# Block inverses of a gated delta rule: DMA re-layout replaced by VectorE's 32x32 transposes, and the order of queued matmuls written down

## The chip, the cores and the metric

One core of one Trainium2 chip runs the whole program in a single launch. The metric is the device time of one execution in microseconds. The kernel before took 2575.57 us (median of 3 runs, 2575.21 to 2578.09).

## The reference

Two layers over 512 latent tokens and 256 context tokens, model width 1024. Each layer: a modulated RMS norm, one input projection of 7696 columns, three mixers that run on its output (a gated convolution with 31 taps, neighbourhood attention, and a bidirectional gated delta rule, "GDN"), a gated merge with an output projection, then a second norm and a convolutional FFN of width 2816. What the change touches is the GDN's triangular solve:

```
lmat  = where(strict, (k*beta) @ k.T * decay, 0)        # decay = exp(g_i - g_j), lower triangle
sol   = triangular_solve(lmat, [v*beta, k*beta*exp(g)], lower=True, unit_diagonal=True)
a     = where(incl, q @ k.T * decay, 0)
# then a scan over chunks with the state s; both directions; 4 heads of 128
```

The kernel works with chunks of 128 tokens, so it has 6 chunks, 2 directions and 4 heads: 48 unit triangular matrices of 128x128 per layer. It inverts them explicitly.

## The kernel before

**Numbers.** Weights and activations of the large projections are split into a rounded high part and a low rest (fp32r, `whi`/`wlo` and `hl`/`ol`), and every product is three matmuls. A weight unit is fetched by SP (`raw`), rounded by ScalarE (`whi`, line 131) and subtracted by VectorE (`wlo`, line 132; the function `wunit`). Two raw and three high and low buffers rotate, so the rounding of a unit waits until TensorE has used the unit three before it.

**Order of a layer.** First the output gate and the decays' projection (`og_first` in layer 0, `og_proj` in layer 1), then `gates`, `gdn_proj` (q, k, v), then two calls of `gdn_core`, one for each pair of heads, then attention, merge, output projection and FFN.

**Queued work.** The projections of attention (`na_units`), of the convolution (`conv_a_proj`) and of the merge gate (`mg_units`) are generators in a queue. The code of the serial parts calls `fill(us)` between its steps, which issues queued matmuls of about that many nominal microseconds (columns x matmuls / 2400) from the queue; the constants stand in the table `FILL`, one row a layer. What is not used up there is issued later, in `finish`. The framework orders each engine's instructions at compile time; `tc.issue_after(ins)` makes the instructions of a block stand behind `ins` on the same engine, and without it a queued matmul may stand earlier or later than where it is written.

**GDN of one pair.** `gdn_core` loads rows of cumulated decays (`D`, lines 897 to 902), forms on VectorE the differences with the column and on ScalarE the exponential, multiplies the products `kk` with beta and decay into `E` (line 913; 24 matrices of 128x128: 12 a direction) and `qk` with decay into `Am`. `gdn_inverse` (line 1022) then inverts all 24. The four diagonal blocks of 32x32 of each are inverted by forward substitution with one matrix per partition: 4 x 12 = 48 matrices of the forward direction in partitions 0 to 47 and 48 of the backward direction, flipped, in 64 to 111. To bring a block of 32 partitions into one partition it goes through HBM: 4 DMAs write the blocks of `E` to `d_e` (line 1032), two read them back (1033, 1034), one loads identities (1036). 31 steps of two VectorE instructions follow (1042, 1044). Then two ScalarE copies with transposed reading (1047, 1048), a flip, four DMAs out (1051, 1052) and eight back (`Td`, line 1059, and the diagonal of `E`, line 1060). Matmuls then combine blocks of 32 to 64 (`iy`, `it`, `ir`, lines 1070 to 1083) and of 64 to 128 (1102, 1111), with evictions between and `fill` calls behind: `sub` behind the substitution, `y32`, `t32`, `y64`, `t64` behind the later steps.

**Taps.** The 31-tap convolution is 120 VectorE instructions `ca` (line 520) a layer, written in the attention's loop and tied behind marks: the first ones behind the end of a substitution, the rest behind the end of the second `gdn_core`.

**Norms.** `norm_mean` sums squares by matmuls of one column and takes a reciprocal square root in eleven small VectorE instructions; `norm_row` spreads it over partitions by matmuls; `norm_scale` and `norm_shift` apply it. Where a second stream's loop runs, `norm_apply` returns the steps as a list (`late`), and the loops take one a step.

## Time and profile before

| | |
|---|---|
| median of 3 runs | 2575.57 us (2575.21 to 2578.09) |
| the profiled execution | 2584.95 us, span 2583.2 us |
| mean granted TensorE clock | 0.982 |
| TensorE / VectorE / ScalarE busy | 96% / 72% / 42% |
| DMA | 356.74 MB, 138 GB/s on average |

The profile is of one execution. Busy is the share of the span in which an engine had an instruction; TensorE's clock is granted at full speed (2.4 GHz) or half of it, and a stretch's value is the mean of the two. A wait is put down to what ended last before the instruction could start.

### The profile page before, as it was taken

The page shows a single profiled execution, that of the slowest core. Times are in us where ns is not written, and L with a number is a line of the kernel's source. Part 1 is how long each engine was busy: PE and PEld are TensorE (multiplying, and loading weights), DVE is VectorE, ACT ScalarE, POOL GpSimd, SP SyncE. Part 2 cuts the span into 40 slices and gives each one's busy share as a digit, 9 for nine tenths or more (in the row PEclk, how much of TensorE's full clock was granted, in tenths as well). Part 3 has the DMA queues.
Part 4 walks back from the last instruction along what each step waited for, and adds up shares of the span by engine and source line. Part 5 has one row for each costly group of instructions (what it writes and reads, how often), then busy time and mean ns, then how long its engine had stood idle before and what let it go on. Part 6 is the DMA issues. An engine that isn't in the chain of part 4 may idle for free. (4 is left out here: it accounts for less than half of the span.)

```text
span 2583.2 us, 42109 instructions
## 1 busy us (share of the span) xinstructions
PE 2484.5 (96%) x16079; PEld 2160.4 (84%) x16079; DVE 1865.7 (72%) x4138; ACT 1072.2 (42%) x2159; POOL 8.5 (0%) x32
## 2 busy tenths in 40 slices
PE   6999999999999999999999999998988999999999
PEld 4988898977778888888888898888877778888887
DVE  5686478799679989877666578876767968755463
ACT  4574343455332344223233346634344544533242
POOL 0000000000000000000000000000000000000000
PEclk9999999999999999999999989998999999999999
DMA  7224434263458554444432342343446276323322
GB/s 254 93 82 127 133 101 139 95 210 103 147 189 265 186 160 134 132 143 129 153 120 89 119 147 83 133 131 109 145 124 216 90 238 203 126 90 99 97 98 90
DMA packets 206762, 356.74 MB, mean 138 GB/s; under 512 B 54320, under 2 KB 102688, under 8 KB 206432
## 3 DMA queue, kind: packets, MB, share of 16 engines
q1 hardware_dynamic: 181664, 320.97, 39.1%
q10 hardware_dynamic: 24896, 33.09, 3.6%
q8 instruction: 126, 2.06, 0.3%
q14 instruction: 76, 0.62, 0.1%
HBM read 297.31 MB, written 56.68 MB: 137 GB/s over the span
## 5 line engine op out<-in xcount | busy, mean ns | idle before, releaser
L131 ACT CAST whi<-raw 128x1024 fp32r<-128x1024 f32 (+2 forms) x319 | 331.6, 1040 | 564.0 <-PE dn L151 202.1
L132 DVE TENSOR_TENSOR wlo<-raw,whi 128x1024 fp32r<-128x1024 f32 (+2 forms) x319 | 385.4, 1208 | 188.1 <-ACT whi L131 185.3
L151 PE MATMUL upl<-hl,whi 128*128 128x512 f32 (+1 forms) x728 | 279.0, 384 | 2.9 <-ACT whi L131 2.0
L151 PE MATMUL upl<-ol,whi 128*128 128x512 f32 (+1 forms) x728 | 279.2, 384 | 0.0
L151 PE MATMUL upl<-hl,wlo 128*128 128x512 f32 (+1 forms) x728 | 278.4, 383 | 0.3 <-DVE wlo L132 0.3
L520 DVE SCALAR_TENSOR_TENSOR ca<-yp,caw,ca 128x783 f32<-128x783 f32 (+1 forms) x240 | 213.0, 887 | 8.1 <-ACT ca L513 6.0
L449 PE MATMUL pjl<-hl,whi 128*128 128x512 f32 x512 | 210.2, 411 | 4.1 <-ACT whi L131 4.1
L449 PE MATMUL pjl<-ol,whi 128*128 128x512 f32 x512 | 206.4, 403 | 0.0
L449 PE MATMUL pjl<-hl,wlo 128*128 128x512 f32 x512 | 204.7, 400 | 0.5 <-DVE wlo L132 0.5
L151 PEld LDWEIGHTS upl<-hl,whi 128*128 128x128 f32 x728 | 137.3, 189 | 28.7 <-ACT whi L131 2.2
L151 PEld LDWEIGHTS upl<-hl,wlo 128*128 128x128 f32 x728 | 137.2, 189 | 27.3 <-DVE wlo L132 0.5
L151 PEld LDWEIGHTS upl<-ol,whi 128*128 128x128 f32 x728 | 137.4, 189 | 25.1 <-DVE ol L324 0.2
L151 PE MATMUL dn<-fhl,wlo 128*128 128x512 f32 x352 | 139.5, 396 | 0.0
L151 PE MATMUL dn<-fll,whi 128*128 128x512 f32 x352 | 139.5, 396 | 0.0
L151 PE MATMUL dn<-fhl,whi 128*128 128x512 f32 x352 | 139.2, 396 | 0.0
L449 PEld LDWEIGHTS pjl<-hl,whi 128*128 128x128 f32 x512 | 97.5, 190 | 25.3 <-ACT whi L131 6.1
L246 DVE CUSTOM_DVE_ANT_1 aj<-at,crows,par 128x512 f32<-128x512 f32 x128 | 93.5, 748 | 33.4 <-DMA at<-ada_t 22.3
L449 PEld LDWEIGHTS pjl<-hl,wlo 128*128 128x128 f32 x512 | 97.4, 190 | 21.2 <-DVE wlo L132 0.9
L585 PE MATMUL na<-wlo,hl 128*128 128x256 f32 x384 | 110.0, 287 | 4.8 <-DVE wlo L132 2.6
L449 PEld LDWEIGHTS pjl<-ol,whi 128*128 128x128 f32 x512 | 97.8, 191 | 19.2 <-issue 0.8
L585 PE MATMUL na<-whi,ol 128*128 128x256 f32 x384 | 110.1, 287 | 0.0
L585 PE MATMUL na<-whi,hl 128*128 128x256 f32 x384 | 109.8, 286 | 0.0
(405 smaller groups left out, 6454.3 us busy)
## 6 DMA issues: line engine op xcount, KB each, us to landing
raw<-w_b SPq DMA_DIRECT2D x88, 512.0 KB
raw<-f_up SPq DMA_DIRECT2D x88, 512.0 KB
at<-ada_t SPq DMA_DIRECT2D x160, 256.0 KB
raw<-w_o SPq DMA_DIRECT2D x32, 512.0 KB
raw<-f_dn SPq DMA_DIRECT2D x32, 448.0 KB
raw<-w_a SPq DMA_DIRECT2D x24, 512.0 KB
mg<-mge ACTq DMA_DIRECT2D x48, 256.0 KB
raw<-w_br SPq DMA_DIRECT2D x24, 512.0 KB
```

What stands on the lines that cost most here:

```text
L131: self.nc.scalar.copy(hi[:, :n], r[:, :n])
L132: self.split = self.nc.vector.tensor_sub(lo[:, :n], r[:, :n], hi[:, :n]).ins
L151: self.nc.tensor.matmul(o, wk[a], x[k][b], start=(k == 0 and i == 0), stop=(k == n - 1 and i == 2))
L246: V.tensor_tensor_reduce(p, w, self.crows[:, r, 4 * h:4 * h + 4], 1.0, m if h else self.p(l, "adab")[:, t:t + 1], ALU.mult, ALU.add, accum ...
L449: self.nc.tensor.matmul(o, wk[a], x[k][b], start=(k == 0 and i == 0), stop=(k == n - 1 and i == 2))
L520: nc.vector.scalar_tensor_tensor(a, y[:, k:k + n], w[:, 31 * c + k:31 * c + k + 1], a, ALU.mult, ALU.add)
L585: self.nc.tensor.matmul(ps[:, :256], x[k][a], wk[b], start=(k == 0 and j == 0), stop=(k == 7 and j == 2))
```

## The change

In the inverse, no DMA is left. `V.transpose` transposes blocks of 32x32 between partitions and elements, so a block of `E` is brought into "one matrix per partition" by one block transpose of each group of 32 partitions (the backward direction; the forward direction by a ScalarE copy, so that both become lower triangular) and one transpose of the whole tile. The identities come from two memsets. After the substitution two transposes give both layouts of the inverse, `X` and `Yt`, which the matmuls of the 32-to-64 step read directly, with a step of 32 elements; the diagonal of `E` is filled by eight VectorE copies. `norm_row` is put behind the last matmul like `norm_mean`. The 31 steps are as before, on 128 partitions. The steps of 32 and of 64 run in two halves of six chunks each, each followed by a fill `inv`. All these matmuls, the fills `inv` and the norms' matmuls are issued in written order (`behind`). The fill behind the substitution is 40 for the first pair of heads and 31 for the second. Decay differences and the transposes of `E` are tied behind the weight split before the last. The ring of large tiles grows from 3 to 5. In layer 0's gate four blocks of matmuls stand before the context norm's mean, three before its row, and the other five behind; in layer 1's gate the context tokens' 16 columns come last, from small tiles that GpSimd copies. The norms' late steps come one step later.

```
-FILL = (dict(e=3.5, sub=37.6, y32=1.6, t32=2.5, y64=1.3, t64=1.0, ...),
-        dict(e=4.1, sub=38.3, y32=1.0, t32=2.5, y64=1.69, t64=1.7, ...))
+FILL = (dict(e=3.5, sub=(40.0, 31.0), inv=0.9, t64=1.0, ...),
+        dict(e=4.1, sub=(40.0, 31.0), inv=0.9, t64=1.7, ...))
...
     def wunit(self, src, n):
         self.nc.scalar.copy(hi[:, :n], r[:, :n])
+        self.before = self.split
         self.split = self.nc.vector.tensor_sub(lo[:, :n], r[:, :n], hi[:, :n]).ins
...
     def norm_mean(self, st):
-        for t in range(nt):
-            nc.tensor.matmul(ps[:, t:t + 1], ...)
+        with self.behind():
+            for t in range(nt):
+                nc.tensor.matmul(ps[:, t:t + 1], ...)
...
-        return [lambda: self.norm_mean(st), head] + [lambda k=k: one(k) for k in range(2, 8)]
+        return [lambda: self.norm_mean(st), lambda: self.norm_row(st)] + [lambda k=k: one(k) for k in range(8)]
+
+    def norm_late(self, late, m):
+        for f in ([], late[:1], late[1:3], late[3:4], late[4:5], late[5:6], late[6:7], late[7:8])[m]:
+            f()
...
+    def behind(self):
+        eng = self.nc.tensor.engine
+        last = next((i for i in reversed(self.nc.cur_bb.bb.instructions) if i.engine == eng), None)
+        return self.tc.issue_after(last) if last is not None else ExitStack()
...
     def og_first(self):
-        mm(0, 2, 4, 8)
+        for i, t in ((0, 2), (0, 3), (0, 4), (0, 5)):
+            mm(i, t, 4, 8)
         self.norm_mean(st)
-        mm(0, 3, 4, 8)
+        mm(1, 2, 4, 8)
+        mm(1, 3, 4, 8)
+        mm(1, 4, 0, 8)
         self.norm_row(st)
...
+        for i, t in ((1, 5), (0, 0), (0, 1), (1, 0), (1, 1)):
+            mm(i, t, 0, 8)
...
     def og_proj(self):
+        small = [self.hp.tile([128, 8, 16], F32R, name="wb" + n) for n in "hl"]
+        units = [self.wunit(self.A["w_g0"][self.l, h], 1088) for h in range(2)]
+        for h in range(2):
+            for a, b in zip(small, units[h]):
+                nc.gpsimd.tensor_copy(a[:, 4 * h:4 * h + 4, :], b.rearrange("p (k c) -> p k c", c=272)[:, :, 256:272])
...
+            for t, k0, k1 in ((2, 0, 8), (3, 0, 8), (4, 0, 4), (5, 0, 4), (4, 4, 8), (5, 4, 8)):
...
+        for t in range(2):
+            ps = self.acc("og")
+            self.og_mm(ps, 0, t, lambda k, a, b: tuple(x[:, k, :] for x in small), 0, 8)
+            self.og_out(ps, 0, t)
...
     def gdn_core(self, pr):
-                D = gp.tile([128, 1024], F32, tag="D", name="D", bufs=3)...
+                D = gp.tile([128, 1024], F32, tag="D", name="D", bufs=5)...
-                for t in range(6):
-                    V.scalar_tensor_tensor(D[:, t, :], ...)
+                with tc.issue_after(self.before):
+                    for t in range(6):
+                        V.scalar_tensor_tensor(D[:, t, :], ...)
...
     def gdn_inverse(self, E, pr):
-        for b in range(4):
-            nc.sync.dma_start(de[b].rearrange("u (j i) -> j u i", i=32), E[32 * b:32 * b + 32, :, 32 * b:32 * b + 32])
-        nc.sync.dma_start(Eb[0:48], de[:, 0:12, :])
-        nc.sync.dma_start(Tf[64:112], de[:, 12:24, :])
-        V.tensor_copy(Eb[64:112], Tf[64:112, ::-1])
-        nc.sync.dma_start(Tt[0:112], self.A["eye32"][0:112])
+        nc.gpsimd.memset(cube(Db)[:, :, 24:32], 0.0)
+        nc.gpsimd.memset(W, 0.0)
+        nc.gpsimd.memset(W[:, ::33], 1.0)
+        for q in qs:
+            with self.tc.issue_after(self.before):
+                V.transpose(cube(Db)[q, :, 12:24].rearrange("p i u -> p u i"), E[q, 12:24, q])
+            S.copy(cube(Db)[q, :, 0:12].rearrange("p i u -> p u i"), E[q, 0:12, q])
+        V.transpose(Z, Db)
...
-        self.fill(FILL[self.l]["sub"])
-        S.copy(Mv[0:48], Tv[0:48].rearrange("p i c -> p c i"))
-        S.copy(Mv[64:112], Tv[64:112].rearrange("p i c -> p c i")[:, ::-1, ::-1])
-        V.tensor_copy(Tf[64:112], Tt[64:112, ::-1])
...
+        self.fill(FILL[self.l]["sub"][pr])
+        X, Yt = sq("X"), sq("Yt")
+        V.transpose(X, W)
+        V.transpose(cube(Yt), Wv.rearrange("p i c -> p c i"))
+        inv, ivt = (cube(Yt), cube(X)), (cube(X), cube(Yt))
...
+        def wait():
+            with self.behind():
+                self.fill(FILL[self.l]["inv"])
+
+        for u0, u1 in halves:
+            yb = self.bank("iy")
+            with self.behind():
...
+                            T.matmul(yb[...], blk(s, 12 * d + u, t), inv[d][qs[s], :, 12 * d + u], start=True, stop=True)
+            S.activation(Y1[:, 32 * u0:32 * u1], yb[:, 0:192], AF.Copy, scale=-1.0)
+            wait()
+        for b, q in enumerate(qs):
+            S.copy(TA[q, ...], inv[b // 2][q, :, ...].rearrange("p i u -> p u i"))
+            for d in range(2):
+                us = slice(12 * d, 12 * d + 12)
+                V.tensor_copy(E[q, us, q], ivt[d][q, :, us].rearrange("p i u -> p u i"))
...
     def out_proj(self):
                 if late:
-                    late.pop(0)()
+                    self.norm_late(late, m)
...
+            for f in late[8:]:
+                f()
...
     def ffn(self):
-                    then = [{6: mean}, {4: head}, {0: lambda: [f() for f in rest]}]
+                    then = [{7: mean}, {6: lambda: [f() for f in (row, *rest[:2])]}, {0: lambda: [f() for f in rest[2:]]}]
```

## Rows read from the trace of the kernel before

**Rows 1.** The page: each engine's busy time, share of span, instructions.

```profile
PE 2484.5 (96%) x16079; PEld 2160.4 (84%) x16079; DVE 1865.7 (72%) x4138; ACT 1072.2 (42%) x2159; POOL 8.5 (0%) x32
```

**Rows 2.** Waits, all engines: who for whom, total us, times, longest.

```profile
DVE wlo L132 <- ACT whi L131: 185.3, 105, 11.7
...
PE iy L1070 <- DMA Td<-e: 15.3, 6, 4.5
```

**Rows 3.** Stretches from the last `E` product to each inverse's end.

```profile
core 0: us, PE busy (x) PEld busy (x) DVE busy (x) ACT busy (x) POOL busy (x), PEclk, DMA share, GB/s
231.80:325.00 93.20, 85.00 (x860) 78.03 (x859) 43.70 (x100) 30.25 (x57) 0.00 (x0) 0.96 0.47 138
381.00:460.00 79.00, 73.39 (x786) 67.91 (x785) 62.32 (x123) 25.81 (x46) 0.00 (x0) 0.96 0.49 142
1680.30:1764.00 83.70, 70.36 (x745) 65.48 (x744) 49.72 (x104) 29.65 (x55) 0.00 (x0) 0.86 0.50 143
1816.00:1906.00 90.00, 82.43 (x719) 69.70 (x717) 58.10 (x119) 28.98 (x44) 0.15 (x2) 0.96 0.52 158
```

**Rows 4.** Stretches: first inverse's substitution; fourth's before, during, behind it.

```profile
245.50:280.10 34.60, 33.81 (x217) 30.29 (x217) 28.52 (x73) 8.86 (x13) 0.00 (x0) 1.00 0.36 120
...
1816.00:1834.00 18.00, 17.09 (x117) 15.61 (x116) 6.22 (x17) 3.04 (x6) 0.00 (x0) 1.00 0.53 146
1834.00:1864.30 30.30, 30.30 (x155) 25.90 (x154) 28.11 (x70) 8.54 (x11) 0.00 (x0) 1.00 0.43 148
1864.30:1882.30 18.00, 13.51 (x61) 10.87 (x60) 16.42 (x23) 8.06 (x8) 0.00 (x0) 0.97 0.55 157
```

**Rows 5.** Chain that ended last, fourth inverse: start us, us, what.

```profile
1869.44 9.45 DMA e<-Tf
...
1878.95 3.26 DMA Td<-e
```

**Rows 6.** Single tiles and lines: xcount, ns min/median/max, first to last start, forms.

```profile
L1035 DVE COPY Eb<-Tf x4: 691/691/691, 244.3 to 1833.3; 48x1024 f32<-48x1024 f32 x4
...
L1047 ACT COPY Eb<-Tt x4: 2090/2126/2149, 280.2 to 1864.4; 48x1024 f32<-48x1024 f32 x4
...
L131 ACT CAST whi<-raw x319: 929/1048/1111, 25.9 to 2562.2; 128x1024 fp32r<-128x1024 f32 x141, 128x896 fp32r<-128x896 f32 x16, 128x1088 fp32r<-128x1088 f32 x3
...
L132 DVE TENSOR_TENSOR wlo<-raw,whi x319: 1078/1221/1289, 27.1 to 2563.2; 128x1024 fp32r<-128x1024 f32 x141, 128x896 fp32r<-128x896 f32 x16, 128x1088 fp32r<-128x1088 f32 x3
...
L1091 DVE COPY E<-ir x16: 545/553/565, 314.5 to 1901.2; 32x384 f32<-32x384 f32 x16
```

**Rows 7.** Stretches from the second inverses of both layers to attention's end.

```profile
442.00:531.00 89.00, 82.38 (x832) 75.30 (x831) 68.69 (x156) 37.47 (x112) 0.20 (x3) 0.95 0.44 138
531.00:680.00 149.00, 147.05 (x1046) 116.55 (x1048) 141.12 (x307) 77.79 (x186) 0.41 (x6) 0.98 0.39 128
1882.00:2060.00 178.00, 165.57 (x1357) 133.38 (x1357) 143.26 (x362) 90.47 (x215) 0.57 (x6) 0.96 0.45 146
```

**Rows 8.** VectorE's lines, 426.4 to 441.6 and 1864.3 to 1882.3: xcount, busy us, mean.

```profile
L520 DVE SCALAR_TENSOR_TENSOR ca<-yp,caw,ca 128x783 f32<-128x783 f32 x11 | 11.4, 1033 | 0.3
...
L520 DVE SCALAR_TENSOR_TENSOR ca<-yp,caw,ca 128x512 f32<-128x512 f32 x19 | 14.3, 751 | 0.6
```

**Rows 9.** Stretches around the gate projections of layers 0 and 1.

```profile
45.00:66.00 21.00, 16.02 (x105) 15.46 (x106) 19.19 (x58) 11.47 (x27) 0.00 (x0) 0.84 0.24 82
1523.00:1545.00 22.00, 20.87 (x122) 20.64 (x123) 12.18 (x34) 11.76 (x18) 0.00 (x0) 0.69 0.22 72
```

**Rows 10.** TensorE: lines of 1897 to 1899.5, and timeline starts in 246.8 to 248.3.

```profile
L1083 PE MATMUL ir<-E,Y 32*32 32x32 f32 x96 | 1.6, 195 | 0.3 <-issue 0.3
...
246.87 0.40 PE L449 MATMUL pjl<-hl,whi 128*128 128x512 f32 x1
...
247.93 0.40 PE L449 MATMUL pjl<-hl,whi 128*128 128x512 f32 x1
```

More of the change, by code (lines that the diff above doesn't have):

```diff
@@ L67, in __init__ @@
         self.tc, self.nc, self.A, self.out = tc, tc.nc, A, out
[L68 removed]
+        self.queue, self.live, self.primed, self.late, self.split = deque(), None, None, [], None
     def run(self):
@@ new lines, in og_proj @@
+        units = [self.wunit(self.A["w_g0"][self.l, h], 1088) for h in range(2)]
+        for h in range(2):
+            for a, b in zip(small, units[h]):
+                nc.gpsimd.tensor_copy(a[:, 4 * h:4 * h + 4, :], b.rearrange("p (k c) -> p k c", c=272)[:, :, 256:272])
+        mean, row, *rest = self.late
+        for i in range(2):
+            wd = 256 if i else 272
+            if i:
+                units = [first, self.wunit(self.A["w_g1"][self.l, 1], 1024)]
+            w = lambda k, a, b: tuple(x[:, wd * (k % 4) + a:wd * (k % 4) + b] for x in units[k // 4])
+            ps = {}
+            for t, k0, k1 in ((2, 0, 8), (3, 0, 8), (4, 0, 4), (5, 0, 4), (4, 4, 8), (5, 4, 8)):
+                if k0 == 0:
+                    ps[t] = self.acc("og")
+                self.og_mm(ps[t], i, t, w, k0, k1)
+                if k1 == 8:
+                    self.og_out(ps[t], i, t)
+                if i == 0 and (t, k0) == (2, 0):
+                    first = self.wunit(self.A["w_g1"][self.l, 0], 1024)
+                    mean()
+                elif i == 0 and (t, k0) == (4, 0):
+                    row()
+                    for f in rest[:4]:
+                        f()
+                elif i == 0 and (t, k0) == (4, 4):
+                    for f in rest[4:]:
@@ new lines, in wait @@
+        def wait():
[3 more added lines that the diff above has]
+            yb = self.bank("iy")
+            with self.behind():
+                for u in range(u0, u1):
+                    for d in range(2):
+                        for s, t in prs[d]:
+                            T.matmul(yb[32 * t:32 * t + 32, 32 * (u - u0):32 * (u - u0) + 32], blk(s, 12 * d + u, t),
+                                     inv[d][qs[s], :, 12 * d + u], start=True, stop=True)
+            S.activation(Y1[:, 32 * u0:32 * u1], yb[:, 0:192], AF.Copy, scale=-1.0)
+            wait()
@@ new lines, in gdn_inverse @@
+        for b, q in enumerate(qs):
+            d = b // 2
+            S.copy(TA[q, :, 32 * (b % 2):32 * (b % 2) + 32], inv[d][q, :, 12 * d:12 * d + 12].rearrange("p i u -> p u i"))
+            for d in range(2):
+                us = slice(12 * d, 12 * d + 12)
+                V.tensor_copy(E[q, us, q], ivt[d][q, :, us].rearrange("p i u -> p u i"))
+        for u0, u1 in halves:
+            tb, rb = self.bank("it"), self.bank("ir")
+            with self.behind():
+                for u in range(u0, u1):
+                    c = 32 * (u - u0)
+                    for d in range(2):
+                        for s, t in prs[d]:
+                            if s // 2 == d:
+                                T.matmul(tb[32 * t:32 * t + 32, c:c + 32], dia(t, d, u), Yq(t, u),
+                                         start=True, stop=True)
+                            T.matmul(rb[32 * s:32 * s + 32, c:c + 32], Yq(t, u), dia(t, d, u), start=True, stop=True)
+            S.copy(TA[32:64, u0:u1, 0:32], v(tb[32:64, 0:192]))
+            S.copy(TA[64:96, u0:u1, 32:64], v(tb[64:96, 0:192]))
```

158 lines of the change are left out of this document (55 added, 103 removed).

## The prediction

> **What bounds the kernel now.** I read the page first. TensorE is busy 96% of the span and VectorE 72% [rows 1], so a change pays only where it takes away TensorE's idle time or its time at the lower clock; a shorter chain on another engine is worth nothing while TensorE has queued matmuls to run. Next I read TensorE's waits [rows 2]: the largest one inside the layers is `iy` waiting for the tile `Td` by DMA, 15.3 us in 6 waits. Then I cut one stretch around each of the four inverses (two head pairs in each of two layers), from the last product that fills `E` to the end of the inverse [rows 3]. There TensorE is idle 93.2-85.0 = 8.2, 79.0-73.4 = 5.6, 83.7-70.4 = 13.3 and 90.0-82.4 = 7.6 us, 34.7 in all. The granted clock was 0.96, 0.96, 0.86 and 0.96, so parts of these stretches ran at 1.2 instead of 2.4 GHz; span times the missing share is 3.7 + 3.2 + 11.7 + 3.6 = 22.2 us. The four inverses hold 56.9 us of lost time, and that is what this change can reach. (Idle time at the lower clock is counted twice in this, a few us.)
>
> The fourth inverse shows the parts [rows 4]: 18.0 us from `E` to the first substitution step, 30.3 us of substitution, in which TensorE never stops, and 18.0 us from there to `iy`, in which it idles 4.5. The chain names those last 18 us [rows 5]: 9.45 us until `e<-Tf` landed, then 3.26 us for `Td<-e`.
>
> **The change, part by part.**
>
> *The inverse's DMAs.* Gone per inverse are 19 DMAs through SP (4 out of `E`, 3 into the working tiles, 4 out, 8 back), the DMA round trip ahead of the substitution and the one behind it. SP's queue loses them too, and the weight loads behind them no longer wait for their turn. In their place stand, on VectorE, four 32-row block transposes of 384 elements, one full transpose (`Z`), the same 62 steps, and two full transposes (`X`, `Yt`); on ScalarE four copies of 384. No row shows a VectorE transpose. From below it is a plain copy of 1024 elements, 0.69 us; from above twice a `wlo` subtraction of 1.22 us [rows 6]. I take 1.22, the nearest full-size row that is not a bare copy. The four of 384 I take at the 0.55 us of the `E<-ir` copies. Before the substitution that is 4 x 0.55 + 1.22 = 3.4 us on VectorE (18.0 now), behind it 2 x 1.22 = 2.4 (18.0 now). Both pieces of the chain shrink by some 14 us.
>
> Most of that is not time: TensorE was at work for 17.1 + 13.5 of those 36 us anyway. What counts is whether the queued work, now held in a written order, covers the new chain. The new chain of the fourth inverse is 3.4 + 30.3 + 2.4 = 36 us. The cover is 40 nominal us for the first pair and 31 for the second. A unit of 0.96 nominal us (three matmuls of 512 and three of 256 columns) takes 247.93-246.87 = 1.06 us [rows 10], so they are 44 and 34 us, plus some 2 us left of the fill ahead of it. The first pairs are covered, the second pairs short by 0 to 3 us. What is late next is the split in front of a step on VectorE, not a DMA.
>
> Behind `iy` there are six places where TensorE waits for an eviction; each has a fill of 0.9, one unit of about 1.06 us. An eviction of half a bank costs under 0.55 us [rows 6]; one split in front of it makes 1.8, so that about every second place leaves 0.7: 2 us an inverse. The diagonal copies into `E` (8 x 0.55 = 4.4 us on VectorE) and eight half evictions (at most 0.55, I take 0.38: 3.0) have four units and the matmuls, some 8 us, to hide under; cover gone, they cost what lies over 8.
>
> So the 15.3 us of DMA waits go, of the other 19.4 us (the small waits between the stages, and splits that came late) I keep 12. The lower clock stands where the long waits stand, the third inverse with most of both; with these gone I keep 5 of 22.2. Gain 56.9-17 = **-40 us** (bounds -50 and -20; the worse case is a rival).
>
> *Strided operands.* `iy` and `ir` now read their moving operand, `it` its weights, with a step of 32 elements. 144 such matmuls of `it` and `ir` took 1.6 us, 11 ns each, at full clock [rows 10]. No row shows one with a step. Below: 0. Above: twice, 240 x 11 ns = 2.6 us an inverse, 11 in all. ScalarE's copy with that step took 2.13 us for 1024 elements against 1.05 for `whi` [rows 6], but the four-quadrant matmul takes its columns more slowly than ScalarE its elements, so I take **+4**. The Trainium skill's page "SBUF — State Buffer", section "Door 1: The DMA port swizzle", says that SBUF is read in lines of 16 bytes and that an access which crosses to a new line each time pays for it, which speaks against this change. ScalarE's 2.13 against 1.05 us agrees; for VectorE and TensorE no run here shows it. By that rule all strided copies and matmuls would double, which is a rival below.
>
> *VectorE's time.* Added per inverse: 2.2 + 3.7 + 4.4 + 3.0 = 13.3; gone: two copies 1.4 and four evictions 2.2. Net +9.7 us (bounds 5 and 18). It also loses the idle time behind the substitution, where 11 taps (11.4 us) ran in the second inverse and 19 (14.3 us) in the fourth [rows 8]. These 21.1 and 24.0 us must fit between there and the end of attention, where VectorE now has 89.0-68.7 + 149.0-141.1 = 28.2 us free in layer 0 and 178.0-143.3 = 34.7 in layer 1 [rows 7]. They fit if two thirds of the gaps can be used; if half, 7.0 + 6.6 us are over. I take **+8** (bounds 0 and 45; TensorE can pull queued units forward, which favours the low end).
>
> *Decays and `E` transposes tied behind a split.* They wait at most as long as that split: `wlo` waited for `whi` 185.3/105 = 1.8 us on average, 11.7 at worst [rows 2]. Queued behind them are the products into `E`; the fill of 3.5 or 4.1 covers the average. I take 0 (bounds -3, where splits come earlier for it, and +8).
>
> *Queues.* The ring of five tiles instead of three lets decay rows and `tk` load earlier. Two more memsets run on GpSimd, idle all along: 0.
>
> *Layer 0's gate.* Between 45 and 66 us TensorE idles 5.0 us, at a clock of 0.84 (3.4 us) [rows 9]. The new order puts 48 matmuls of 256 or 272 columns between the mean and the row (0.12 us each at the rate of rows 10, 5.7 us in all, more than the whole idle time), and 24 behind the row: **-6** (0 to -8).
>
> *Layer 1's gate.* Between 1523 and 1545 us it idles 1.1 us and runs at a clock of 0.69, 6.8 us [rows 9]; 48 matmuls of 16 columns stand among the wide ones there. They move to the end: **-5** (+2 to -8).
>
> *Norms.* The mean and row come one step later and in written order. Gains of a wait or two against a root's chain that now holds TensorE if VectorE is late: **-1** (-4 to +5).
>
> Sum: -40 + 4 + 8 + 0 - 6 - 5 - 1 = -40 us. The profiled execution took 2584.95 us, of which 2583.2 is span; it becomes 2545. The median of the timed runs is 9.4 us lower, 2575.57, so **2536**. With the near bounds of each term the likeliest case reaches from 2516 to 2556.
>
> **The rivals.**
>
> *Slower: the written order holds TensorE.* `iy` now stands behind the last queued unit, and nothing else may run while `Yt` is missing. For it: splits in the substitution's stretch wait for TensorE in turn, and it took 34.6 us in the first inverse [rows 4]. With ScalarE's strided price (384 elements 0.8 us, four of them), 34.6 and 2.4 + 1.2 behind it the chain is 42.6 against 36 in the second pairs, 6.6 us; with a split and a late eviction at each of the six places, 1.2 each, 7.4 an inverse. Idle 43 us, with the clock's share as now (22.2/34.7) 70 against 56.9: +13, with +4, +8 and nothing gained at the gates **2601**. It decides from 8.7 us of idle time an inverse. Against it: 31 of the 36 us of chain are steps whose pace is known.
>
> *Only the DMA waits go.* The 15.3 us and a like part of the clock, 9.8, vanish, the small waits stay under other names, the gates give nothing: -25 + 12 = **2562**. For it: most of the shortened chain was already covered.
>
> *VectorE becomes the bound in attention.* It is busy 141 of 149 us there in layer 0 [rows 7]. If none of the gaps can be used, 45 us come back and the kernel stays at **2573**. Against it: taps have until the last units of the queue.
>
> *Strided operands cost double on every engine*, as they do on ScalarE. The transposes of 384 and `Yt` grow by 4 x 0.45 + 1.2 = 3.0, uncovered in two pairs: 6. The diagonal copies grow by 3.6 to 8.0, with the evictions 11 over a cover of 8: 3 each, 12. The matmuls 7 more. +25, **2561**. (It is the rule of the page named above.) Against it: no row shows it for VectorE or TensorE.
>
> *The change does not do what it says:* splits stand ahead of every transpose, the 56.9 us stay, and strides and taps eat what the gates give: **2576**.
>
> **How the numbers follow.** Forecast 0.58, strides 0.08, only the DMA waits 0.14, VectorE's bound 0.06, no effect 0.03, slower 0.11. A run of this kernel tells 0.2% (5.2 us) from no change. Faster by more than that: the first three and a third of the fourth, 0.82; within: two thirds of the fourth and part of the fifth, 0.06; slower 0.12. The range, 2514 to 2574, leaves out the slow case and a few hundredths below.
>
> **What would show it.** Right: no `Td` wait; TensorE idle under 4 us in each inverse; a granted clock of 0.98 and more there; transposes of 1024 elements near 1.2 us; the mean clock of the run above 0.982. Wrong: an `iy` wait on `Yt` of several us in the second pairs; taps that end later and TensorE idle in attention; `it` and `ir` far over 1.6 us.

## The result, and the profile after

| | before | after |
|---|---|---|
| median of the timed runs, us | 2576.83 (2575.21 to 2580.65, 4 runs) | 2556.27 (2555.27 to 2560.03, 4 runs) |
| ratio, 95% interval | | 0.9922 (0.9908 to 0.9936) |
| profiled execution, us | 2584.95 | 2555.27 |
| mean granted clock | 0.982 | 0.989 |
| DMA, MB / packets | 356.74 / 206762 | 345.46 / 167369 |

The change makes the kernel 20 us faster, half of the 40 that were forecast. The answer to [rows 1] is the page's first section after: TensorE's busy time is 10 us lower (part of it is matmuls that no longer run at half clock), VectorE's is 34 us higher.

```profile
PE 2474.3 (97%) x16079; PEld 2142.5 (84%) x16079; DVE 1899.8 (74%) x4204; ACT 1076.8 (42%) x2179; POOL 11.9 (0%) x44
```

TensorE's waits after (who for whom, total us, times, longest), to be read beside [rows 2]: no wait for `Td` is left and `iy` hardly waits at all (1.4 us). In its place stand waits for weight splits (`wlo`), for ScalarE's `nsq` and for attention's probabilities (`P`). The line above these is the start of the program (`nps`), as in the kernel before.

```profile
...
PE PT L1280 <- DVE P L1273: 9.5, 8, 4.9
PE na L593 <- DVE wlo L133: 6.1, 2, 4.9
...
PE na L593 <- ACT nsq L599: 4.6, 1, 4.6
PE pjl L457 <- ACT whi L131: 4.4, 5, 1.0
PE pjl L457 <- DVE wlo L133: 3.7, 4, 1.9
```

The windows view of the four inverses after. They are cut from the first product `kk`, since new gaps stand ahead of the last `E`, where [rows 3] begin, to the last copy into `E`. Stretch, its length, busy time of TensorE, its weight loads, VectorE, ScalarE and GpSimd, then TensorE's clock, DMA share and rate.

```profile
199.50:282.50 83.00, 75.41 (x784) 68.27 (x783) 64.80 (x163) 31.28 (x58) 2.10 (x4) 0.96 0.41 133
336.80:408.60 71.80, 66.85 (x763) 62.33 (x763) 66.15 (x154) 26.88 (x52) 1.86 (x3) 0.95 0.34 112
1639.80:1721.00 81.20, 75.38 (x830) 70.83 (x829) 72.78 (x171) 34.40 (x64) 2.10 (x4) 0.96 0.45 148
1773.10:1853.40 80.30, 76.39 (x745) 65.86 (x745) 70.93 (x161) 29.69 (x52) 1.85 (x3) 0.96 0.37 122
```

TensorE still idles 7.6 + 5.0 + 5.8 + 3.9 = 22.3 us there, and the missing clock is worth 3.3 + 3.6 + 3.2 + 3.2 = 13.3: 35.6 us of lost time, where the prediction kept 17 of 56.9. (Cut from `kk` as well, the kernel before had 35.1 and 21.0.) Of the idle time 5.8 us lie ahead of the last `E`, outside the prediction's rows; in the kernel before it was 0.4 us there. Cut at the last `E` like [rows 3], the four idle times are 3.8, 4.2, 4.5 and 3.9 us, at clocks of 0.94, 0.94, 0.94 and 0.95.

The two longest gaps, 4.90 and 4.62 us, stand at the first pairs of the two layers. Where the first comes from is seen on VectorE's timeline at the first inverse (start, us, engine, line, operation, out<-in).

```profile
206.73 3.24 DVE L929 SCALAR_TENSOR_TENSOR D<-D,G,km 128x128 f32<-128x128 f32 x12 [1.78 <-PE na L593]
209.88 2.23 DVE L941 SCALAR_TENSOR_TENSOR E<-kk,beta,D 128x128 f32<-128x128 f32 x8
...
214.93 3.23 DVE L929 SCALAR_TENSOR_TENSOR D<-D,G,km 128x128 f32<-128x128 f32 x12
218.07 2.15 DVE L941 SCALAR_TENSOR_TENSOR E<-kk,beta,D 128x128 f32<-128x128 f32 x8
...
221.34 1.12 DVE L941 SCALAR_TENSOR_TENSOR E<-kk,beta,D 128x128 f32<-128x128 f32 x4
...
222.70 1.22 DVE L133 TENSOR_TENSOR wlo<-raw,whi 128x1024 fp32r<-128x1024 f32 x1
...
224.50 3.42 DVE L1065 STREAM_TRANSPOSE Db<-E 32x384 f32<-32x384 f32 x4
...
228.28 1.24 DVE L1067 STREAM_TRANSPOSE Z<-Db 128x1024 f32<-128x1024 f32 x1
...
229.74 0.19 DVE L1072 TENSOR_TENSOR Tm<-Z,W 128x31 f32<-128x31 f32 x1
```

From the first decay difference to the first substitution step VectorE works 23 us without a pause. The split that TensorE needs next had its rounded part at 210.22 and stands behind all of `D` and `E` and most of `A`, to 222.70. TensorE ran dry at 219.07 and waited 4.90 us. Near the end of the wait the clock falls to 1.2 GHz: from 223 to 230 us the granted clock is 0.51. In the kernel before, a split stood inside the second group of decay differences (224.06), and behind the last `E` the inverse's first DMA trip left VectorE a pause of 7.5 us, so that the next split ran as soon as its `whi` was there:

```profile
222.15 1.65 DVE L901 SCALAR_TENSOR_TENSOR D<-D,G,km 128x128 f32<-128x128 f32 x6
...
224.06 1.21 DVE L132 TENSOR_TENSOR wlo<-raw,whi 128x1024 fp32r<-128x1024 f32 x1
225.23 1.66 DVE L901 SCALAR_TENSOR_TENSOR D<-D,G,km 128x128 f32<-128x128 f32 x6
...
233.03 1.22 DVE L132 TENSOR_TENSOR wlo<-raw,whi 128x1024 fp32r<-128x1024 f32 x1
...
242.97 1.23 DVE L132 TENSOR_TENSOR wlo<-raw,whi 128x1024 fp32r<-128x1024 f32 x1 [7.51 <-ACT whi L131]
```

The gap of 4.62 us in layer 1 is put down to another engine. TensorE waits there for ScalarE's `nsq`, which reads an accumulator of attention's projection (`na`). ScalarE has it behind the four copies of `E` that the change gave it, and these wait for VectorE's `E` first:

```profile
1661.70 3.38 ACT L1066 COPY Db<-E 32x384 f32<-32x384 f32 x4 [2.64 <-DVE E L941]
1665.10 0.38 ACT L599 ACTIVATE nsq<-na 128x256 f32<-128x256 f32 x1
```

```profile
1665.54 0.58 PE L593 MATMUL na<-whi,hl 128*128 128x256 f32 x1 [4.62 <-ACT nsq L599]
```

The second and the fourth inverse have no such gap, and a stretch at 1.2 GHz all the same, from 390.3 to 397.2 and from 1806.9 to 1813.7. The one begins amid a wait of 1.4 us, with one of 1.2 us just before, the other amid a wait of 1.9 us.

Span by stage, after minus before, between the same instructions of the two profiles: to the first `kk` -7.3; from there to layer 0's merge -5.3 (558.7 to 553.4); merge and FFN -2.4; layer 1's gate and q, k, v -2.1; its inverses and attention -13.4 (436.3 to 422.9); the rest +0.8. The sum is -29.7, the difference of the two profiled executions.

### The profile page after: what moved, and what is told of

The parts are those of the page before. It is cut to its first block, busy times and chain, and to the rows that moved or that the text cites. A ratio compares the mean times of both kernels' runs of the same rounds, so it can differ in the third digit from the quotient of the medians.

```text
span 2553.5 us, 42053 instructions
## 1 busy us (share of the span) xinstructions
PE 2474.3 (97%) x16079; PEld 2142.5 (84%) x16079; DVE 1899.8 (74%) x4204; ACT 1076.8 (42%) x2179; POOL 11.9 (0%) x44
## 2 busy tenths in 40 slices
DMA packets 167369, 345.46 MB, mean 135 GB/s; under 512 B 16528, under 2 KB 64896, under 8 KB 167040
## 4 chain that ended last, share of the span: by engine, by line
PE 72%; DVE 15%; DMA 7%; ACT 3%; issue 2%; SPq 0%; ACTq 0%; DVEq 0%; POOL 0%; POOLq 0%
PE upl L152 19%; PE dn L152 12%; PE pjl L457 7%; PE pjl L152 5%; PE upc L152 5%; PE mbl L152 4%; PE na L593 4%; DVE ca L528 3%; DVE wlo L133 2%; PE pjc L152 2%; PE og L627 2%; PE wo L152 2%; PE pjc L457 2%; DMA mg<-mge 2%; PE mbc L152 1%
```

## The experiments

Each ratio is to runs of the kernel before that were timed beside it, with its 95% interval. The medians of these lay between 2575.97 and 2580.71 us, so 0.001 is 2.6 us. A kernel's executions spread by up to 21 us.

### Parts of the change, and both kernels again

Both kernels as they are; then the change cut in two. `gates_norms` keeps the inverse by DMA:

```
+        with self.behind():                             # gates_norms: norm_mean, norm_row
+    def norm_late(self, late, m):                       # and the loops that call it
+        for i, t in ((0, 2), (0, 3), (0, 4), (0, 5)):   # og_first's order
+        small = [self.hp.tile([128, 8, 16], ...)]       # og_proj's order
```

`inverse_only` is the rest of the change's diff (inverse, fills, its written order, ring, ties).

> The kernel before, unchanged, profiled once more. Theory 'the offset belongs to one execution': the 9.4 us by which the profiled execution of before (2584.95 us) stood above its median is a half-clock phase or two that this execution had and others don't have, so a new profiled execution lies within 5 us of the median, 2572 to 2582, with a mean granted clock nearer 0.986 than 0.982. Rival 'profiling always costs this kernel 9 us': 2583 to 2587 again, at a clock of 0.982.

> The kernel after, unchanged, so that it stands on the same chip and beside the same runs as the others of this call. Theory 'the first pair of medians is right': 2554 to 2560, 0.992 of before. Rival 'the first four runs were lucky': 2560 to 2566.

> The kernel before with only the new order of the gates' and norms' matmuls, the inverse by DMA as before. By the prediction's terms (layer 0's gate 6, layer 1's gate 5, norms 1) 12 us faster than before: 2565. By the stages of the two traces (7.3 in layer 0's gate, 2.4 in layer 0's FFN, 2.1 in layer 1's gate) also some 12, but with layer 1's half clock still there. If so the inverse's part of the change is worth only 2565-2556 = 9 us of the predicted 40 - 4 - 8 = 28. Rival 'the parts need each other': alone it gives 4 us or less, 2572 and up, and the inverse's part is worth the rest.

> The kernel before with only the new inverse (transposes, fills, written order, ring, ties); gates and norms as before. By the prediction's terms (-40 for the DMAs, +4 for strides, +8 for VectorE) 28 us faster than before, 2550. If the parts add up, with gates and norms worth 3 alone and the whole change worth 20, it is 17 to 19 us faster, 2559 to 2561. Rival 'the parts need each other': 10 us or less, 2568 and up, and gates and norms give the rest only beside the new inverse.

| | median, us | ratio |
|---|---|---|
| before, profiled once more | 2588.14 (one) | |
| after again | 2561.59 | 0.9930 (0.9915 to 0.9944) |
| gates and norms alone | 2575.06 | 0.9990 (0.9975 to 1.0006) |
| inverse alone | 2563.63 | 0.9954 (0.9937 to 0.9971) |

The kernel after is 18 to 20 us faster. Its second median, 2561.59, lies in the range of the rival, but the kernel before was slower beside it too, and the two ratios agree within their intervals. The inverse alone gives 12 us (8 to 16), not 28; gates and norms alone 3 (at most 6), not 12, though the first `kk` comes 7.1 us earlier in their profile too. The halves add up to 14.5; beside the whole's 18 to 20 that is within the intervals, and whether they need each other stays open. The inverse was not cut further: no run has the transposes without the written order and the new fills, or these with the DMAs, so how the 12 us divide between them is not shown. The second profile of before (2588.14) missed its expectation: it lies 10 us above the median again. It is no price of profiling that every kernel pays, since the profiles of after (2555.27 and 2554.72) are the lowest times of their groups; whether the kernel before pays it each time, two profiles do not settle.

### The gap at the first pairs: tie, ring, VectorE's load

`ring3`, `no_tie`, `no_a` (zeros for `Am`) and `d_gp`:

```
-gp.tile([128, 1024], F32, tag="D", ..., bufs=5)      # ring3, at all places
+gp.tile([128, 1024], F32, tag="D", ..., bufs=3)
-with tc.issue_after(self.before):                    # no_tie, D and transposes
-V.tensor_tensor(Am[...], qk[...], Ds[d][...], ALU.mult)   # no_a
+Gp.memset(Am, 0.0)
-V.scalar_tensor_tensor(D[:, t, :], ..., ALU.subtract, ALU.min)   # d_gp
+Gp.tensor_tensor(D, D, self.G[...].to_broadcast(...), ALU.subtract)
+Gp.tensor_tensor(D, D, mk[d]...to_broadcast(...), ALU.add)
```

> The kernel after with the ring of large tiles back at three instead of five. Theory 'the ring makes the burst': with three tiles the decay rows of the second head must wait for a free tile, so that a weight split stands between the two groups of decay differences of each first pair, as it did before the change. TensorE's gaps at the first pairs (4.90 us and 4.62 us, each with a half-clock phase of 6.83 us) shrink below 2 us, and the time falls by 8 to 14 us to 2542 to 2549. Rival 'the gap only moves': the queued work in front of the substitution is the same, TensorE runs out a few microseconds later, and the time stays within 4 us of 2556. Second rival 'the ring pays elsewhere': the decay rows and token tiles of the second pairs come late with three tiles, and the kernel is 3 to 10 us slower than after, 2559 to 2566.

> The kernel after without the tie of decay differences and block transposes behind the weight split before the last. Theory 'the ring makes the burst': VectorE's order at the first pairs is the same without the tie, only the second pairs' decay differences move ahead of attention-side steps of the recurrence, so the time stays within 4 us of after, 2552 to 2560, and the gaps of 4.9 and 4.6 us stay. Rival 'the tie makes the burst': the gaps of the first pairs go and the time falls by 10 us or more. Second rival 'the tie protects the splits of the second pairs': 4 to 10 us slower than after, up to 2566.

> The kernel after without the products of qk with the decays (8 instructions, 4.05 us an inverse, on VectorE ahead of the inverse); Am is zeros from GpSimd, so the output lacks that part. Theory 'the stretch from the first product into E to iy is set by VectorE's unbroken chain': the chain is 4 us shorter in each of four inverses, the late splits come 2 to 4 us earlier, and the time falls by 10 to 16 us against after, 2540 to 2546. Rival 'the gap only moves': TensorE has the same queued work, comes to iy earlier or waits at another split, and the time falls by less than 6 us, 2550 and up.

> The kernel after with the decay differences (12 instructions of 0.27 us for each direction and head on VectorE, 6.5 us an inverse) on GpSimd, as two instructions of 768 elements each (the mask is added instead of taken as a minimum). Theory 'VectorE's unbroken work ahead of the substitution makes the splits late': the splits now come before or among the products into E, TensorE's gaps of 4.9 and 4.6 us at the first pairs shrink below 2 us, and the time falls by 8 to 16 us, 2540 to 2548. Rival 'the work is short, not the split': gaps of 3 us or more stay, and the time is within 4 us of 2556. Second rival: GpSimd needs over 3 us a tile or slows VectorE beside it, so that E comes later: 2558 to 2566.

| | median, us | ratio |
|---|---|---|
| ring of three | 2560.39 | 0.9928 (0.9913 to 0.9943) |
| no tie | 2562.96 | 0.9943 (0.9929 to 0.9957) |
| no `A` products | 2559.38 | 0.9919 (0.9903 to 0.9935) |
| decay differences on GpSimd | 2574.32 | 0.9981 (0.9968 to 0.9995) |

My theory that ring or tie makes the gap fell. Without the tie VectorE's order at layer 0's first pair is the same, and the gaps stay; the time is 4 us above after, inside the intervals. With the ring of three a split does stand inside the second group of decay differences again, and the time doesn't move: TensorE's waits show the idle time in other places, 4.56 us for `nsq` at 227 and twice 4 us at `iy`.

```profile
PE iy L1105 <- DVE Yt L1079: 8.1, 2, 4.1
...
PE pjc L457 <- ACT nsq L599: 4.6, 1, 4.6
```

Without the `A` products (4 us of VectorE an inverse) the two gaps shrink to 1.80 and 2.33 us, so both follow from VectorE's chain into `E`; and the time is still only 2 us lower, within the intervals. On GpSimd the decay differences take 1.47 and 1.84 us an instruction, and a split beside them is slowed: the split's row at the first pair (count, ns min/median/max, first to last start).

```profile
L133 DVE TENSOR_TENSOR wlo<-raw,whi x2: 2525/2710/2894, 208.6 to 211.7; 128x1024 fp32r<-128x1024 f32 x2
```

Against 1.22 us otherwise. So `E` comes no earlier, TensorE waits 6.96 us for `Yt`, and the kernel loses 14 us against after.

### What a trip through HBM is worth

`hop_front` puts one trip back ahead of the substitution, `hop_back` behind it.

```
 V.transpose(Z, Db)
+nc.sync.dma_start(self.d_h, Z)        # hop_front
+nc.sync.dma_start(Z, self.d_h)
...
+nc.sync.dma_start(self.d_h, W)        # hop_back
+nc.sync.dma_start(W, self.d_h)
 V.transpose(X, W)
```

> The kernel after with one trip through HBM put back ahead of the substitution: Z (128x1024) is written out and read back by SP's queue, two DMAs an inverse, some 5 us of latency by the 3.26 and 9.45 us of the old chain. Theory 'the trips were covered by queued matmuls and gave VectorE time for splits': four trips cost less than 6 us in all, within 6 us of after, and TensorE's gap at the first pairs shrinks or stays. Rival 'the chain sets iy': each trip costs its latency, 4 x 4 to 5 us, so 14 to 20 us slower than after.

> The same trip put back behind the substitution (W is written out and read back before the two transposes). Theory 'the chain sets iy, the trip behind the substitution is what was paid': TensorE reaches iy 0 to 2 us after Yt now, so each trip of about 5 us leaves 3 to 5 us of idle time in front of iy, 12 to 20 us in all with the clock, 2570 to 2578. Rival 'the gap only moves': TensorE's idle time grows by less than 2 us an inverse because less is lost elsewhere, within 6 us of after.

Both came out slower than the kernel before: 2586.74 us, 1.0029 (1.0016 to 1.0042), and 2587.67, 1.0029 (1.0016 to 1.0042). Against after (0.9926, the mean of its two) that is 0.0103, 26.6 us, or 6.6 us a trip. The chain of `hop_front` at the first inverse (start, us, what) shows the trip:

```profile
227.72 1.24 DVE Z L1068
...
228.98 3.05 DMA hop<-Z
...
232.11 4.43 DMA Z<-hop
...
236.63 0.22 DVE Tm L1075
```

In `hop_back` the same two take 5.02 and 4.17 us:

```profile
258.69 5.02 DMA hop<-W
...
263.73 4.17 DMA W<-hop
```

And TensorE pays in front of `iy`, where it waits 25.6 us in all in the one and 25.1 in the other (1.4 in after):

```profile
PE iy L1108 <- DVE Yt L1082: 25.6, 4, 10.4
```

```profile
PE iy L1108 <- DVE Yt L1082: 25.1, 4, 7.7
```

So with the new order the trip ahead of the substitution is not covered, against my theory, and the one behind it costs more than I gave it: the chain sets `iy`, and each trip costs nearly its latency of 7.6 to 9.3 us.

This is the price of a trip in the new order, not what the old trips cost. The kernel before makes two trips an inverse and is faster than both of these kernels, which make one; and taking all eight out, with all else that changed in the inverse, gave 12 us and not eight times 6.6. In the old order most of both trips was covered: in [rows 4] TensorE is at work for 30.6 of the 36 us around them.

### More cover, and VectorE in attention

`e5` makes the fills between the products into E longer; `taps_half` leaves out the odd taps in after, `before_taps_half` in before, `e5_taps_half` does both; `d_gp_e5` is `d_gp` with the fills of `e5`. The half-tap kernels do not compute the whole convolution.

```
-dict(e=3.5, ...), dict(e=4.1, ...)          # e5
+dict(e=5.0, ...), dict(e=5.6, ...)
 with self.tc.issue_after(m):                # the half-tap kernels: only for even k
     nc.vector.scalar_tensor_tensor(a, y[:, k:k + n], ...)
```

> The kernel after with the fill between the products into E raised from 3.5 and 4.1 to 5.0 and 5.6 us. Theory 'no cover ahead of the inverse': VectorE needs 15.7 us from the decay differences to the last product into E and then 7 us to the first substitution step, all in one piece, and TensorE's four fills don't cover it; four fills longer by 1.5 us each give 6 us more, the gaps of 4.9 and 4.6 us at the first pairs and the half clock behind them go, and the time falls by 8 to 14 us, 2542 to 2548. Rival 'the split is late, not the work': the added units need splits which stand behind the same VectorE work, so the gaps stay within 2 us and the time within 4 us of 2556. Second rival 'paid back later': the chain into E waits for the longer fills, the queue is empty earlier, and the time is 3 to 8 us longer, 2559 to 2564.

> Both: decay differences on GpSimd and the longer fills of 5.0 and 5.6 between the products into E. If late splits and missing cover both count, this is the fastest, 2536 to 2544. If only the split counts, it equals the one with GpSimd alone within 3 us. If the longer fills hold up the chain into E, it is 3 to 8 us above that one.

> The kernel after without the odd taps of the 31-tap convolution: 60 instructions of about 1.04 us a layer are left out on VectorE, 62 us a layer, and its output is not the convolution's. Theory 'VectorE bounds the stretch from the first product into E to the merge': TensorE's idle time of 21.1 and 22.0 us there falls below 14 in each layer and the time falls by 15 to 30 us against after, 2526 to 2541. Rival 'the order of the work and the waits at the splits bound it, VectorE's sum does not': within 6 us of after, 2550 to 2558.

> The kernel before without the same odd taps (output not the convolution's). Read as the difference to the kernel after with half the taps. Theory 'VectorE takes back what the DMAs gave': with VectorE relieved the change is worth 28 to 36 us instead of 20, so this one lies 28 to 36 us above the other. Rival 'nothing is taken back, the DMA waits were worth that little': the difference stays 18 to 24 us. Here the taps filled VectorE's idle time behind the substitution, so that leaving them out gains less: 0 to 8 us against before.

> Fills of 5.0 and 5.6 between the products into E, and the odd taps of the convolution left out (60 VectorE instructions a layer, output not the convolution's). The longer fills cost 16 us with all taps and half the taps gained 13 us with the old fills (2548). Theory 'the longer fills cost because the taps on VectorE are late in layer 1's attention': without half of them the 12.25 us wait for the tap results goes, and the time is 2540 to 2550, as with the old fills or less. Rival 'the queue is used up too early, taps or not': 2558 to 2568.

| | median, us | ratio |
|---|---|---|
| longer fills | 2577.37 | 0.9999 (0.9985 to 1.0012) |
| longer fills, D on GpSimd | 2583.04 | 1.0033 (1.0016 to 1.0049) |
| after, half the taps | 2548.48 | 0.9879 (0.9866 to 0.9892) |
| before, half the taps | 2572.19 | 0.9968 (0.9957 to 0.9980) |
| longer fills, half the taps | 2551.28 | 0.9890 (0.9868 to 0.9911) |

Six more microseconds of cover in each pair cost 19 us instead of gaining 8: the whole gain of the change. On top of `d_gp` they cost 13. The queued units used there are missing in layer 1's attention, which has 797 matmuls in `e5` and 844 in after. TensorE's waits of `e5` begin with the convolution's result, which VectorE's taps hold up (0.8 us at most in after):

```profile
PE lnT L545 <- DMA lnx<-ca: 14.8, 2, 12.2
```

The same stage (layer 1, attention to merge) in `e5`, and then in after:

```profile
1930.40:2078.90 148.50, 121.79 (x797) 92.53 (x798) 112.66 (x295) 67.97 (x147) 0.26 (x2) 0.92 0.43 145
```

```profile
1925.40:2062.70 137.30, 128.42 (x844) 97.19 (x845) 109.31 (x281) 69.32 (x147) 0.27 (x2) 0.99 0.48 160
```

TensorE idles 26.7 us there instead of 8.9, at a clock of 0.92. With half the taps the longer fills cost 0.0011, 3 us and by the intervals no more than 9, so late taps make most of the 19. And half the taps (62 us of VectorE in layer 0; 45 in layer 1, where one takes 0.75 us) are worth 12 us in after, between theory and rival there, and 8 in before. With VectorE relieved the change is worth 0.0089, 23 us, instead of 18 to 20. That is in the range of the rival, by which VectorE takes nothing back: some 4 us by the medians, which the intervals do not tell from none.

### Split, chain and cover together

`d_act` takes the decay differences off VectorE with less of GpSimd; `sub45` raises the cover behind the substitution of layer 0's first pair; `d_act_s45` does both.

```
-V.scalar_tensor_tensor(D[:, t, :], ..., ALU.subtract, ALU.min)     # d_act
-S.activation(D, D, AF.Exp)
+Gp.tensor_tensor(D, D, mk[d]...to_broadcast(...), ALU.add)
+S.activation(D[:, t, :], D[:, t, :], AF.Exp, bias=self.nG[...])      # nG is -G
-dict(e=3.5, sub=(40.0, 31.0), ...)                                 # sub45
+dict(e=3.5, sub=(45.0, 31.0), ...)
```

> The decay differences off VectorE: GpSimd adds the mask (one instruction of 768 elements for each direction and head, 2.0 us), ScalarE subtracts the column as the bias of the exponential (six instructions instead of one). VectorE's chain ahead of the inverse is 6.5 us shorter and the splits stand before the products into E. Theory 'split and chain are co-bound, both at once pay': 8 to 16 us faster than after, 2543 to 2552. Rival 'idle time only moves, whatever is relieved': within 4 us of after, as with the other three.

> The kernel after with the fill behind the substitution of layer 0's first pair raised from 40 to 45 us, nothing else. Theory 'co-bound': TensorE comes to iy 1.7 us after Yt already, so more cover alone only moves iy 5 us later; the time stays within 4 us of after, or is up to 4 us longer. Rival 'cover is what is missing': 4 us or more faster than after.

> d_act (decay differences on GpSimd and ScalarE) with the fill behind the substitution of layer 0's first pair raised from 40 to 45 us. Theory 'co-bound: earlier split, shorter chain and cover together pay': the wait of 5.98 us for Yt and the half clock at it go, 4 to 9 us faster than d_act, 2549 to 2554. Rival 'the five microseconds are then missing in attention, where VectorE sets the pace': within 3 us of d_act, 2555 to 2561.

| | median, us | ratio |
|---|---|---|
| `d_act` | 2557.94 | 0.9915 (0.9895 to 0.9936) |
| `sub45` | 2565.47 | 0.9944 (0.9922 to 0.9966) |
| `d_act_s45` | 2559.01 | 0.9918 (0.9895 to 0.9942) |

In `d_act` the waits of 4.9 and 4.6 us are gone, one of 5.98 us for `Yt` has come, and the time is that of after, as the rival has it:

```profile
PE iy L1104 <- DVE Yt L1078: 6.0, 1, 6.0
```

`sub45` alone is 5 us above after, inside the intervals. `d_act_s45` clears the wait for `Yt` too: in the first inverse TensorE idles 2.9 us from `kk` to `iy`, at full clock. But the time doesn't follow. TensorE's waits now begin with attention:

```profile
PE PT L1279 <- DVE P L1272: 14.0, 5, 6.2
...
PE lnB L559 <- DVE xn L555: 7.0, 4, 3.3
```

Layer 0 cut at the merge's first matmul, from the first `kk` to there and from there to layer 1, in after and then in `d_act_s45`:

```profile
199.50:753.00 553.50, 532.38 (x4268) 467.84 (x4267) 431.55 (x1067) 233.99 (x559) 4.86 (x17) 0.98 0.40 130
753.00:1490.40 737.40, 730.17 (x4181) 639.34 (x4181) 563.30 (x1139) 252.76 (x381) 0.15 (x2) 1.00 0.47 150
```

```profile
199.10:749.10 550.00, 526.71 (x4268) 462.62 (x4267) 420.35 (x1012) 242.32 (x598) 21.46 (x25) 0.99 0.40 130
749.10:1493.40 744.30, 735.24 (x4182) 642.52 (x4181) 566.70 (x1145) 252.97 (x382) 0.16 (x2) 0.99 0.48 150
```

In these two profiles 3.5 us are gained ahead of the merge and 6.9 lost behind it. The time is the rival's (within 3 us of `d_act`), but its reason, that the five microseconds of queued work are missing later, is not shown: TensorE has the same matmuls on both sides of the cut (4268, and 4181 against 4182). Of the 6.9 us, 1.8 are idle time, with a wait of 3.3 us for the convolution's norm (`xn`), and 5.1 are lower clock, in two stretches; the longer one, at the start of the FFN (937 us), stands in the profiles of before and `d_act` too and not in that of after. None of the three kernels can be told from after, and no kernel here that does the whole work beats it beyond the interval.

## Why the prediction was half right

**Direction and mechanism: right, in the main.** The `Td` waits are gone, the mean clock is 0.989 (over 0.982 was asked), and the inverse alone makes the kernel 12 us faster. TensorE idle under 4 us in each inverse: by the prediction's own cut just missed in two (4.2 and 4.5). A clock of 0.98 there: missed in all four.

**"So the 15.3 us of DMA waits go, of the other 19.4 us I keep 12 ... I keep 5 of 22.2": this term failed.** Kept were 22.3 and 13.3, together 18.6 us more than I kept. The 22.3 are the two gaps at the first pairs (9.5) and 12.8 us of small waits, about the 12 that I had. The 13.3 are one stretch at 1.2 GHz in each inverse, 3.2 to 3.6 us each. "The lower clock stands where the long waits stand" is wrong for two of the four: they begin amid waits of 1.4 and 1.9 us.

The step behind the two gaps is "the first pairs are covered". Cover counts only while its weights are split and its accumulators free. I priced the decay differences' wait for a split at 0 ("the fill of 3.5 or 4.1 covers the average") and had no term for the reverse, a split that stands behind the decay differences and `E`, nor for the pause that VectorE loses with the first DMA trip, nor for an accumulator that ScalarE empties only behind its four new copies. In layer 0 the split came 12.5 us after its `whi`. (The 11.7 us of [rows 2] are the other case: there VectorE was free and the `whi` late.) In layer 1 `nsq` stood behind the copies. Tie and ring themselves can't be told from after (0.9943 and 0.9928), so the 0 for them stands.

The length of the first chain came out by luck. From the prediction's figures it is 3.4 + 34.6 + 2.4 = 40.4 us; measured are 40.8 (222.46 to 263.27), but in parts 7.3, 29.1 and 4.5. The fourth, summed at 36, took 41.4 us (1789.7 to 1831.2).

Second, I took lost time for time that can be reached. Five kernels (`ring3`, `no_a`, `d_gp`, `d_act`, `d_act_s45`) removed, moved or shrank one or both gaps and none is faster than after beyond its interval; the idle time came up at `iy`, at attention's start or behind the merge. Queued units are one stock for inverse, attention and merge, and in `e5` attention waited for VectorE's taps when the stock was used earlier. In these runs it hardly mattered which gap the stock filled. That the shared stock is the reason is argued, not shown. The rival "only the DMA waits go: the small waits stay under other names", at 0.14 and 2562, was nearest: that half of it held. Its reason (most of the shortened chain was already covered) fits the kernel before, as the section on the trips shows; its "the gates give nothing" does not fit layer 0.

**The offset made the other half of the miss.** The terms predict 2545 for the profiled execution and it took 2555.27: 10 us off. The other 10 come from the 9.4 us that I took off because the profile of before stood that far above its median: the profile of after stands 1.0 below its own. Both profiles of before lie 9 to 10 us above the median beside them, both of after below it; whether that belongs to the kernels or to single executions stays open, but it did not carry over.

By the stages of the two profiles the stretches from the first `kk` to the merge gave 18.7 us, where -40 + 4 + 8 = -28 was forecast, and all else 11, where 12 was. So there the miss lies in the inverse's term. Since its lost time fell by 20.5 us (56.1 to 35.6), strides and VectorE together took back some 2 us and not 12, by this rough sum.

**Strides, +4: within its bounds; no run takes them out alone.** From the trace, 48 matmuls `iy` with a moving operand of step 32 take 0.66 us (one every 13.5 ns, from start to start), and 90 dense ones before 0.83 (one every 8.7 ns):

```profile
264.96:265.62 0.66, 0.65 (x48) 0.65 (x48) 1.00 0.73 189
```

```profile
311.12:311.95 0.83, 0.82 (x90) 0.82 (x90) 1.00 0.00 0
```

`it` and `ir` start every 10.9 instead of 9.9 ns. Together that is 0.6 us an inverse, 2.4 in all. On VectorE (tile, count, ns) `X` and `Z` took 1.24, as forecast; the strided `Yt` and `Db` not:

```profile
L1079 DVE STREAM_TRANSPOSE Yt<-W x4: 1974/2044/2152, 261.1 to 1829.1; 128x1024 f32<-128x1024 f32 x4
L1078 DVE STREAM_TRANSPOSE X<-W x4: 1234/1238/1246, 258.8 to 1828.0; 128x1024 f32<-128x1024 f32 x4
...
L1065 DVE STREAM_TRANSPOSE Db<-E x16: 804/863/895, 224.5 to 1793.5; 32x384 f32<-32x384 f32 x16
L1114 DVE COPY E<-X x16: 438/494/525, 263.1 to 1835.0; 32x384 f32<-32x384 f32 x16
```

Four times 0.31 and 0.82 more make 2.1 us of chain. The rule of the Trainium skill's "SBUF — State Buffer", section "Door 1: The DMA port swizzle", that an access which crosses to a new line each time pays, agrees for these transposes (2.04 against 1.24) and not for the copies with the same step (0.49; the dense ones before took 0.55, but read PSUM). The page gives no price for it; "double" was taken from ScalarE's rows.

**VectorE's time, +8: within its bounds of 0 and 45**, some 4 us by the half-tap kernels, whose intervals allow none; VectorE's net load, forecast at 4 x 9.7 = 39 us, is 34. (Two thirds of the gaps are 18.8 and 23.1 us, so the 21.1 and 24.0 do not quite fit them, as the prediction says they do.)

**Gates and norms, -12: too much by the runs.** Layer 0's gate is as forecast. In layer 1 the clock stays low, 0.78 against 0.69. The stretches that answer to [rows 9]:

```profile
42.00:64.00 22.00, 20.69 (x165) 19.36 (x165) 18.54 (x57) 12.89 (x29) 0.00 (x0) 1.00 0.29 95
1509.00:1532.00 23.00, 23.00 (x133) 21.04 (x134) 13.46 (x36) 9.58 (x18) 0.00 (x0) 0.78 0.22 76
```

No idle time is left in the second. The 48 matmuls of 16 columns still stand in it, now in one block from 1516.2 to 1524.2 us, and the clock falls amid them, at 1520.2:

```profile
1516.20:1520.40 4.20, 4.20 (x40) 4.20 (x38) 3.45 (x10) 3.41 (x5) 0.00 (x0) 0.97 0.42 143
1520.40:1524.20 3.80, 3.80 (x16) 3.41 (x15) 0.07 (x1) 0.00 (x0) 0.00 (x0) 0.50 0.17 53
```

So moving them together did not free the clock, and they may be why it falls; no run without them shows it. In time the part gave 3 us alone and 7 beside the new inverse (0.9926 against 0.9954).

**The slower rival** did not come: `iy` waits 1.4 us in all for `Yt`. Its mechanism is real: with a trip put back TensorE waits 25 us at `iy` in the same written order.

## What to carry to other kernels

When a DMA wait goes, ask what another engine did in it: here VectorE split weights in the pause, and the new chain left it 23 us without one. Ask too what the new instructions stand ahead of in their engine's queue: ScalarE's four copies held up an accumulator. Idle time in a stage is not the price of the stage when several stages live on one stock of queued work: here a gap that was filled opened another elsewhere. And a profile's distance from the median should not be carried from one kernel to the next: forecast profile to profile, and widen the range by the spread of the executions.

## What was not expected of the hardware

- A 32x32 block transpose of 128x1024 in fp32 on VectorE takes 1.24 us dense (`X`) and 2.04 with a source step of 32 elements (`Yt`).
- A subtraction of two SBUF tiles on VectorE (1.22 us) takes 2.53 and 2.89 us beside GpSimd's two-input instructions (`d_gp`), 1.75 and 2.33 in `d_act`. The Trainium skill's "SBUF — State Buffer", section "Who interferes with whom", says that a VectorE instruction with two SBUF inputs contends with a GpSimd instruction that reads SBUF; these rows agree.
